# Attention scores from float32r products of split queries and keys, with the mask folded into the rotary product

## The chip, the cores and the metric

The kernel runs on one core of a Trainium2 chip. A core has a matrix engine (TensorE, PE in the profile, with weight loads as PEld), a vector engine (VectorE, DVE), a scalar engine (ScalarE, ACT), a general engine (GpSimd, POOL) and a queue for transfers (SyncE, SP). Each works through its own list of instructions in order and they meet at semaphores. Matrix products accumulate in PSUM, from where DVE or ACT move them to SBUF. The metric is the time of one launch on the device in microseconds.

## What is computed

Two layers of a transformer-like trunk on 256 tokens of 2048 features. Layer 0 is a convolution module and an MLP, layer 1 is latent attention and an MLP. Only the attention of layer 1 is touched. Its core, per block of 128 queries:

```python
s = (jnp.einsum('bqhd,bkhd->bhqk', qn, k_nope)
     + jnp.einsum('bqhr,bkr->bhqk', qp, k_pe)).astype(jnp.float32) * scale
q_chunk = (blk * Q_BLOCK + jnp.arange(Q_BLOCK)) // CHUNK
mask = k_chunk[None, :] <= q_chunk[:, None]
s = jnp.where(mask[None, None], s, -jnp.inf)
p = jax.nn.softmax(s, axis=-1).astype(v.dtype)
return jnp.einsum('bhqk,bkhd->bqhd', p, v)
```

There are 16 heads. A query has a part of 128 (qn) and a rotary part of 64 (qp); keys have a part of 128 per head (k_nope) and one rotary part of 64 that all heads share (k_pe). The mask lets a chunk of 64 queries see its own chunk of keys and the earlier ones, so query block 0 needs 128 keys and block 1 needs 256.

## The kernel before

Everything is float32. A long product is made of three float32r products (`mm3`): a float32r copy of each operand (its high part, written by ACT) and the difference to the original (its low part, by DVE) give high x high + low x high + high x low. Weights arrive by DMA as `raw`, are split by `split_half` in halves (L154 on ACT, L155 on DVE), and a list of units holds the order of all attention weights. `start_unit` notes that a unit has begun and `prefetch` then splits the unit two places ahead and loads one further on. Everything in the attention is issued in an order written out by hand.

The attention goes as follows. First the two down projections (`ckv` with the rotary key, then `cq`). During the second the rotary key is rotated by `rope` on DVE, copied twice side by side and transposed into `kpT` (L1141 to L1156). Then the heads, in four groups of four. The projections of a group are 14 pieces of about 1.4 us on PE each: four for queries (`qn_piece`), two for rotary queries (`qp_piece`, with `rope`), eight for keys and values (`kv_piece`); the pieces of group g+1 are spread over the four heads of group g, where they fill the time in which DVE and ACT do the softmax. `qp_turn` transposes the rotary queries of a group. In the last group, `o_piece` (parts of the output product) fills in instead.

One head in the loop at L1183: `scores` (L1037) makes the score products, the maxima on DVE (L1052, L1053) and the exponentials on ACT (L1055); one piece; `values` of the head before (L1075); `weights` (L1060: reciprocal and scaling on DVE); a prefetch; the other pieces, each with a prefetch; `weights_turn` (L1067), which transposes the probabilities on PE and copies them by ACT. In the scores the operands are plain float32:

```python
nc.tensor.matmul(o, qTs[g][:, i, ts], kTs[g][:, i, :n], start=True, stop=False)
nc.tensor.matmul(o, qpTs[g][half, i // 2, ts], kpT[half, :n], start=False, stop=False)
nc.tensor.matmul(o[:, n - CHUNK : n], mrow, mcol, start=False, stop=True)
```

The third adds -1e30 where the mask forbids, as a bfloat16 product over one partition. PSUM is cut into six accumulators (`acc`) and two tiles for transposes (`tr`), each handed out in turn.

Of the kernel before, what the change touches and what calls it, by code (L numbers as in the profile page):

```python
# [10 lines left out]
F32 = mybir.dt.float32  # L11
# [7 lines left out]
P = 128  # L19
D = 2048  # L20
KC = D // P
T = 2
S = T * P
# [13 lines left out]
PAD_CONST = 24  # L37
PAD_SMALL = 48
PAD_RIGHT = 48
PAD_KV = 40  # L40
PAD_O = 56
WB = 6
LOOK = WB // 2 - 1
# [29 lines left out]
def trunk_kernel(  # L73
# [54 lines left out]
    def nm(s):  # L128
        uid[0] += 1
        return f"{s}_{uid[0]}"  # L130
# [693 lines left out]
    with ExitStack() as cx:  # L824
# [3 lines left out]
        def rope(dst, src, t, nh):  # L828

            a, b = src[:, :, 0:HR], src[:, :, HR:DR]  # L830
            cb = cos[:, t : t + 1, :].broadcast_to([P, nh, HR])
            sb = sin[:, t : t + 1, :].broadcast_to([P, nh, HR])
            m = [at2.tile([P, 4, HR], F32, tag=f"m{i}", name=nm("m"))[:, :nh, :] for i in range(4)]
            nc.vector.tensor_tensor(m[0], a, cb, op=ALU.mult)
            nc.vector.tensor_tensor(m[1], b, sb, op=ALU.mult)
            nc.vector.tensor_tensor(m[2], b, cb, op=ALU.mult)
            nc.vector.tensor_tensor(m[3], a, sb, op=ALU.mult)
            nc.vector.tensor_tensor(dst[:, :, 0:HR], m[0], m[1], op=ALU.subtract)
            nc.vector.tensor_tensor(dst[:, :, HR:DR], m[2], m[3], op=ALU.add)


        mrow = at.tile([1, P], BF16, name="mrow")
        nc.vector.memset(mrow, 0.0)
        nc.vector.memset(mrow[:, 0:CHUNK], 1.0)
        mcol = at.tile([1, CHUNK], BF16, name="mcol")
        nc.vector.memset(mcol, NEG)

        HG = 4
        NG = H // HG
# [77 lines left out]
        kvl = at.tile([P, KR // P, S], F32R, name="kvl")  # L927
        qh = at.tile([P, QR // P, S], F32R, name="qh")
        ql = at.tile([P, QR // P, S], F32R, name="ql")
        kpT = at.tile([P, S], F32, name="kpT")  # L930
        pad_o = at.tile([P, PAD_O], F32, name="pad_o")
        nc.gpsimd.memset(pad_o, 0.0)
        oh = at.tile([P, H, S], F32R, name="oh")
# [18 lines left out]
        gp = []  # L952


        kTs, vvs, qTs, qps, qpTs = {}, {}, {}, {}, {}

        def kv_piece(g, i, c):

            key = ("kvu", g, i)
            if i == 0 and c == 0:  # L960
                kTs[g] = gp[0].tile([P, HG, S], F32, tag="kT", name=nm("kT"))
                vvs[g] = gp[0].tile([P, T, HG * DV], F32, tag="vv", name=nm("vv"))
            if c < 2:
                start_unit(key, c)
            po = acc_tile()
            if c < 2:
                o = po[:, :S]
                ns = slice(c * (DN + DV), c * (DN + DV) + DN)
                for j in range(NJ):
                    wh, wl = w_at(key, j)  # L970
                    nc.tensor.matmul(o, wh[:, ns], kvh[:, j, :], start=j == 0, stop=False)  # L971
                    nc.tensor.matmul(o, wh[:, ns], kvl[:, j, :], start=False, stop=False)  # L972
                    nc.tensor.matmul(o, wl[:, ns], kvh[:, j, :], start=False, stop=j == NJ - 1)  # L973
                nc.scalar.activation(kTs[g][:, 2 * i + c, :], o, AF.Copy)
            else:
                t = c - 2
                ts = slice(t * P, (t + 1) * P)
                o = po[:, : 2 * DV].rearrange("p (h n) -> p h n", h=2)
                for j in range(NJ):
                    wh, wl = (a.rearrange("p (h n) -> p h n", h=2)[:, :, DN:] for a in w_at(key, j))  # L980
                    mm3(o, kvh[:, j, ts], kvl[:, j, ts], wh, wl, j == 0, j == NJ - 1)
                nc.vector.tensor_copy(vvs[g][:, t, 2 * i * DV : 2 * (i + 1) * DV], po[:, : 2 * DV])

        def qn_piece(g, i):
            key = ("qn", g)
            if i == 0:
                qTs[g] = gp[0].tile([P, HG, S], F32, tag="qT", name=nm("qT"))
            if i < 2:
                start_unit(key, i)
            o = acc_tile()[:, :S]  # L990
            ns = slice(i * DN, (i + 1) * DN)
            for j in range(NJ):
                wh, wl = w_at(key, j)
                nc.tensor.matmul(o, wh[:, ns], qh[:, j, :], start=j == 0, stop=False)  # L994
                nc.tensor.matmul(o, wh[:, ns], ql[:, j, :], start=False, stop=False)
                nc.tensor.matmul(o, wl[:, ns], qh[:, j, :], start=False, stop=j == NJ - 1)
            nc.scalar.activation(qTs[g][:, i, :], o, AF.Copy)

        def qp_piece(g, t):
            key = ("qp", g)  # L1000
            start_unit(key, t)
            o = acc_tile()[:, : HG * DR]
            ts = slice(t * P, (t + 1) * P)
            for j in range(NJ):
                wh, wl = w_at(key, j)
                mm3(o, qh[:, j, ts], ql[:, j, ts], wh, wl, j == 0, j == NJ - 1)
            qps[g, t] = at2.tile([P, HG, DR], F32, tag="qp", name=nm("qp"))
            rope(qps[g, t], o.rearrange("p (h n) -> p h n", h=HG), t, HG)

        def qp_turn(g):  # L1010
            pt = tr_tile()
            for t in range(T):
                qp = qps.pop((g, t))
                for i in range(HG // 2):
                    nc.tensor.transpose(
                        pt[:, i * S + t * P : i * S + (t + 1) * P],
                        qp[:, 2 * i : 2 * i + 2, :].rearrange("p a b -> p (a b)"),
                        ident,
                    )
            qpTs[g] = gp[0].tile([P, HG // 2, S], F32, tag="qpT", name=nm("qpT"))  # L1020
            nc.vector.tensor_copy(qpTs[g].rearrange("p a b -> p (a b)"), pt)

        def kv_work(g):
            return [lambda i=i, c=c: kv_piece(g, i, c) for i in range(HG // 2) for c in range(4)]
# [3 lines left out]

        def group_work(g):
            kv = kv_work(g)  # L1030
            return q_work(g) + kv[:3] + [lambda: (qp_turn(g), kv[3]())] + kv[4:]


        sides = [(0, 0, P), (1, P, S)]
# [2 lines left out]
        def scores(h):  # L1037

            g, i = divmod(h, HG)
            half = slice((i % 2) * DR, (i % 2 + 1) * DR)  # L1040
            ss = scs[h] = acc_tile()
            mx = at2.tile([P, T], F32, tag="mx", name=nm("mx"))
            zs = zss[h] = at2.tile([P, T], F32, tag="zs", name=nm("zs"))
            pr = prs[h] = at2.tile([P, 3 * P], F32, tag="pr", name=nm("pr"))
            for t, at_, n in sides:
                o = ss[:, at_ : at_ + n]
                ts = slice(t * P, (t + 1) * P)
                nc.tensor.matmul(o, qTs[g][:, i, ts], kTs[g][:, i, :n], start=True, stop=False)  # L1048
                nc.tensor.matmul(o, qpTs[g][half, i // 2, ts], kpT[half, :n], start=False, stop=False)  # L1049
                nc.tensor.matmul(o[:, n - CHUNK : n], mrow, mcol, start=False, stop=True)  # L1050
            for t, at_, n in sides:
                nc.vector.tensor_reduce(mx[:, t : t + 1], ss[:, at_ : at_ + n], axis=AX.X, op=ALU.max)  # L1052
            nc.vector.tensor_scalar(mx, mx, scalar1=-SCALE, scalar2=None, op0=ALU.mult)  # L1053
            for t, at_, n in sides:
                nc.scalar.activation(  # L1055
                    pr[:, at_ : at_ + n], ss[:, at_ : at_ + n], AF.Exp, bias=mx[:, t : t + 1], scale=SCALE,
                    accum_out=zs[:, t : t + 1],
                )
# [42 lines left out]
        with tc.manual_schedule():  # L1101
# [26 lines left out]
            for k in range(KC):  # L1128
# [9 lines left out]
                if k == 3:  # L1138
                    normed(ckv, KR, sq)
                    kps = []  # L1140
                    for t in range(T):  # L1141
                        kp = at2.tile([P, 2, DR], F32, tag="kp", name=nm("kp"))
                        rope(kp[:, 0:1, :], ckv[:, t : t + 1, KR:], t, 1)
                        nc.vector.tensor_copy(kp[:, 1, :], kp[:, 0, :])
                        kps.append(kp)
                if k == 9:
                    to_T(ckv, 0, kvh_k, kvl_k, g_kv)
                if k == 11:
# [1 line left out]
                if k == 13:  # L1150
                    pt = tr_tile()
                    for t in range(T):
                        nc.tensor.transpose(
                            pt[:, t * P : (t + 1) * P], kps[t].rearrange("p a b -> p (a b)"), ident
                        )
                    nc.vector.tensor_copy(kpT, pt[:, :S])  # L1156
            cq = at.tile([P, T, QR], F32, tag="cx", name="cq")
            for t in range(T):
                nc.scalar.activation(cq[:, t, :], ps[t], AF.Copy, scale=r[:, t : t + 1])
# [15 lines left out]
            work = group_work(1)  # L1175
            warm(AF.Exp)
            work[0]()
            qp_turn(0)
            for w in work[1:3]:
                prefetch(1)  # L1180
                w()
# [1 line left out]
            for g in range(NG):  # L1183
                for i in range(HG):
# [3 lines left out]
                    todo, work = work[:n], work[n:]  # L1188
                    scores(h)
                    todo.pop(0)()  # L1190
                    if h > 0:
                        values(h - 1)
                    weights(h)
                    prefetch(1)
                    for w in todo:
                        w()
                        prefetch(1)
                    weights_turn(h)
                if g + 2 < NG:
                    work = group_work(g + 2)  # L1200
# [60 lines left out]
```

## Time and profile before

| | |
|---|---|
| time, median of 3 runs | 2034.71 us (2034.69 to 2035.07) |
| the profiled execution's own time | 2034.44 us |
| its span, first to last instruction | 2032.6 us |
| granted clock of PE | 0.999 |
| heads, from the first scores to the last | 1118.5 to 1251 us |
| PE records of the scores: L1048, L1049, L1050 | 64, 64 and 32 |
| transposes of the rotary queries, L1015 | 16 |

A line of the time view gives start in us, duration in us, engine, line, operation, output and inputs, shape and count; a bracket at its end is idle time before it and what ended it. Matmuls are pipelined, so their printed durations overlap and the distance of starts is the cost. A float32 product appears as two records and two weight loads, a float32r product as one. The page also names, per group of instructions, busy time, mean duration, and what ended the idle time before them.

### The profile page before, as it was taken

The numbers are of one execution on the slowest core, as the hardware profiler recorded it, in microseconds if no ns is written. First come the engines' busy times: TensorE is split into PE (matmuls) and PEld (weight loads), VectorE is DVE, ScalarE is ACT, GpSimd is POOL, SyncE is SP. The second block draws the span as 40 slices with busy tenths as digits, with TensorE's granted clock in tenths as the row PEclk, the third lists the DMA queues.
The fourth block names the chain that finished last, engine by engine and source line by source line (L and its number), as shares of the span: only waits on it lengthen the run. The fifth ranks groups of instructions, "written<-read, shape, count | busy, mean of one in ns | idle before, by whom it ended". The sixth has DMA issues, their size and how long they took to land.

```text
span 2032.6 us, 27882 instructions
## 1 busy us (share of the span) xinstructions
PE 2009.5 (99%) x11132; PEld 1747.1 (86%) x11132; DVE 1214.8 (60%) x1820; ACT 951.7 (47%) x1325; POOL 174.2 (9%) x101
## 2 busy tenths in 40 slices
PE   7999999999999999999999999999999999999998
PEld 7999888888888888888899887888888888888886
DVE  5999866665544465555446654665564455565454
ACT  5444655544433454444445444554443334454442
POOL 5887400000000000000000000000000000000000
PEclk9999999999999999999999999999999999999999
DMA  7555355665555665555555344566655566655552
GB/s 235 166 167 166 125 186 180 194 187 188 202 189 190 196 193 187 187 193 193 187 162 170 108 139 145 187 207 187 188 196 196 188 196 192 192 187 189 199 192 104
DMA packets 243268, 367.59 MB, mean 181 GB/s; under 512 B 15417, under 2 KB 89793, under 8 KB 242881
## 3 DMA queue, kind: packets, MB, share of 16 engines
q1 hardware_dynamic: 242400, 364.68, 56.0%
q8 instruction: 87, 1.43, 0.3%
q10 hardware_dynamic: 736, 1.12, 0.2%
q14 instruction: 45, 0.36, 0.0%
HBM read 363.68 MB, written 2.10 MB: 180 GB/s over the span
## 4 chain that ended last, share of the span: by engine, by line
PE 98%; DVE 1%; DMA 0%; ACT 0%; issue 0%; SPq 0%; DVEq 0%; ACTq 0%
PE acc L397 23%; PE acc L180 16%; PE acc L182 16%; PE acc L181 16%; PE acc L398 12%; PE acc L482 3%; PE acc L484 3%; PE acc L483 3%; PE sum L515 1%; PE acc L1049 1%; PE tr L237 1%; PE acc L1048 1%; PE acc L971 0%; PE acc L994 0%; PE acc L972 0%; PE acc L973 0%
## 5 line engine op out<-in xcount | busy, mean ns | idle before, releaser
L155 DVE TENSOR_TENSOR lo<-raw,hi 128x1024 fp32r<-128x1024 f32 (+1 forms) x628 | 755.2, 1206 | 685.1 <-ACT hi L154 673.3
L154 ACT ACTIVATE hi<-raw 128x1024 fp32r<-128x1024 f32 (+1 forms) x696 | 722.4, 1046 | 792.0 <-PE acc L181 458.3
L397 PE MATMUL acc<-xt,hi 128*128 128x512 f32 x2048 | 710.5, 390 | 0.0
L398 PE MATMUL acc<-xt,lo 128*128 128x256 f32 x2048 | 577.7, 282 | 0.0
L397 PEld LDWEIGHTS acc<-xt,hi 128*128 128x128 f32 x2048 | 384.4, 188 | 80.5
L180 PE MATMUL acc<-hi,gh 128*128 128x512 f32 x1024 | 398.6, 389 | 0.0
L182 PE MATMUL acc<-lo,gh 128*128 128x512 f32 x1024 | 398.4, 389 | 0.0
L181 PE MATMUL acc<-hi,gl 128*128 128x512 f32 x1024 | 398.4, 389 | 0.0
L398 PEld LDWEIGHTS acc<-xt,lo 128*128 128x128 f32 x2048 | 387.1, 189 | 0.1
L182 PEld LDWEIGHTS acc<-lo,gh 128*128 128x128 f32 x1024 | 192.2, 188 | 40.1
L180 PEld LDWEIGHTS acc<-hi,gh 128*128 128x128 f32 x1024 | 192.2, 188 | 39.7
L181 PEld LDWEIGHTS acc<-hi,gl 128*128 128x128 f32 x1024 | 192.2, 188 | 39.6
L549 DVE SCALAR_TENSOR_TENSOR sum<-ub,w_dw,sum 128x256 f32<-128x256 f32 x402 | 167.7, 485 | 4.9 <-ACT sum L518 2.9
L155 POOL TENSOR_TENSOR lo<-raw,hi 128x1024 fp32r<-128x1024 f32 x68 | 162.1, 2407 | 57.2 <-ACT hi L154 57.2
L482 PE MATMUL acc<-xt,hi 128*128 128x256 f32 x512 | 147.3, 288 | 0.0
L484 PE MATMUL acc<-xt,lo 128*128 128x256 f32 x512 | 143.2, 280 | 0.6 <-POOL lo L155 0.6
L483 PE MATMUL acc<-xt,hi 128*128 128x256 f32 x512 | 143.1, 279 | 0.0
L484 PEld LDWEIGHTS acc<-xt,lo 128*128 128x128 f32 x512 | 96.2, 188 | 0.8 <-POOL lo L155 0.8
L483 PEld LDWEIGHTS acc<-xt,hi 128*128 128x128 f32 x512 | 96.3, 188 | 0.6 <-DVE xt L193 0.2
L482 PEld LDWEIGHTS acc<-xt,hi 128*128 128x128 f32 x512 | 96.3, 188 | 0.4
L925 POOL MEMSET pad_kv<- 128x40 f32 x1 | 0.1, 132 | 772.6 <-PE acc L182 772.6
L405 ACT ACTIVATE v<-acc 128x256 f32<-128x256 f32 x128 | 46.4, 381 | 25.3 <-PE acc L398 25.3
(200 smaller groups left out, 1718.6 us busy)
## 6 DMA issues: line engine op xcount, KB each, us to landing
raw<-in_mlp_w SPq DMA_DIRECT2D x256, 1024.0 KB, 5.2
raw<-in_conv_w_pw SPq DMA_DIRECT2D x64, 512.0 KB, 4.9
raw<-in_conv_w_pw SPq DMA_DIRECT2D x16, 1024.0 KB, 5.1
raw<-in_mla_w_o SPq DMA_DIRECT2D x16, 1024.0 KB, 5.7
raw<-in_mla_w_kv_up SPq DMA_DIRECT2D x8, 1024.0 KB, 5.3
raw<-in_mla_w_in SPq DMA_DIRECT2D x8, 576.0 KB, 3.7
raw<-in_mla_w_in SPq DMA_DIRECT2D x4, 1024.0 KB, 5.0
raw<-in_mla_w_q_up SPq DMA_DIRECT2D x16, 256.0 KB, 3.2
```

Of the source, the lines that this page charges most:

```text
L154: nc.scalar.activation(hi, raw[:, js, :], AF.Copy)
L155: eng.tensor_tensor(lo, raw[:, js, :], hi.bitcast(F32), op=ALU.subtract)
L180: nc.tensor.matmul(ps, sh, mh, start=start, stop=False)
L181: nc.tensor.matmul(ps, sl, mh, start=False, stop=False)
L182: nc.tensor.matmul(ps, sh, ml, start=False, stop=stop)
L397: nc.tensor.matmul(ps[b], wh[:, bs], xhl(k), start=k == 0, stop=False)
L398: nc.tensor.matmul(ps[b][:, :S], wl[:, bs], xh(k), start=False, stop=k == KC - 1)
L405: nc.scalar.activation(v[:, b, :], o[:, S:], AF.Copy)
L482: nc.tensor.matmul(o, wh[:, bs], xh(k), start=k == 0, stop=False)
L483: nc.tensor.matmul(o, wh[:, bs], xl(k), start=False, stop=False)
L484: nc.tensor.matmul(o, wl[:, bs], xh(k), start=False, stop=k == KC - 1)
L549: nc.vector.scalar_tensor_tensor(out=out, in0=ubs[c][:, w : w + S], scalar=tap(c, w), in1=pcs[c], op0=ALU.mult, op1=ALU.add)
```

## The change

- Queries and keys are kept as a high and a low part (`parts_tile`, `in_parts`): the ACT copy out of PSUM now writes float32r, and a DVE subtraction writes the low part. The score product over 128 features becomes an `mm3`.
- The rotary part is stacked on partitions. `kpA` holds the high part of the rotary key twice, `qpA` the high part of the rotary query above its low part, so one product over 128 partitions gives two of the three terms. `kpB` holds the low part of the key in its upper 64 partitions and the mask values in the lower ones; `qpB` holds the high part of the query and the matching ones. Their product gives the third term and the mask. `mrow`, `mcol` and the bfloat16 product go away.
- `kpB` and the two `qpB` get their constant halves at the start of the attention: memsets into `scratch` and nine ACT copies.
- `qp_piece` also splits the rotated queries (`qhl`); `qp_turn` works in two visits of two heads each, with four transposes and two ACT copies per visit; the second visit goes with the next piece.
- In the loop over heads, `values` of the head before moves behind the pieces, to just ahead of `weights_turn`.
- Space: `rope`'s four temporaries have one buffer each, a pad is smaller, and the scratch space for dynamic DMA is cut to 1024 bytes, which shifts other tiles by 15,360 bytes.

```diff
-            m = [at2.tile([P, 4, HR], F32, tag=f"m{i}", name=nm("m"))[:, :nh, :] for i in range(4)]
+            m = [at2.tile([P, 4, HR], F32, tag=f"m{i}", name=nm("m"), bufs=1)[:, :nh, :] for i in range(4)]
...
-        kpT = at.tile([P, S], F32, name="kpT")
+        kpA = at.tile([P, S], F32R, name="kpA")
+        kpB = at.tile([P, S], F32R, name="kpB")
+        qpB = [at.tile([P, HG, S], F32R, name=f"qpB{i}") for i in range(2)]
+        mk, mq = scratch[:, :S], scratch[:, S:]
+        for m in (mk, mq):
+            nc.vector.memset(m[DR:, :], 0.0)
+        for t in range(T):
+            row = slice(DR + t * (P - DR) // 2, DR + t * (P - DR) // 2 + 1)
+            nc.vector.memset(mk[row, (t + 1) * P - CHUNK : (t + 1) * P], NEG)
+            nc.vector.memset(mq[row, t * P : t * P + CHUNK], 1.0)
+        nc.scalar.activation(kpB[DR:, :], mk[DR:, :], AF.Copy)
+        for i in range(2):
+            for j in range(HG):
+                nc.scalar.activation(qpB[i][DR:, j, :], mq[DR:, :], AF.Copy)
...
+        def in_parts(o, parts, i):
+            hi_part(o, parts[0][:, i, :])
+            lo_part(o, parts[0][:, i, :], parts[1][:, i, :])
...
-                nc.scalar.activation(kTs[g][:, 2 * i + c, :], o, AF.Copy)
+                in_parts(o, kTs[g], 2 * i + c)
...
-            nc.scalar.activation(qTs[g][:, i, :], o, AF.Copy)
+            in_parts(o, qTs[g], i)
...
-            qps[g, t] = at2.tile([P, HG, DR], F32, tag="qp", name=nm("qp"))
-            rope(qps[g, t], o.rearrange("p (h n) -> p h n", h=HG), t, HG)
-
-        def qp_turn(g):
+            qp = at2.tile([P, HG, DR], F32, tag="qp", name=nm("qp"))
+            rope(qp, o.rearrange("p (h n) -> p h n", h=HG), t, HG)
+            hl = qps[g, t] = at2.tile([P, HG, 2, DR], F32R, tag="qhl", name=nm("qhl"))
+            hi_part(qp, hl[:, :, 0, :])
+            lo_part(qp, hl[:, :, 0, :], hl[:, :, 1, :])
+
+        def qp_turn(g, m):
             pt = tr_tile()
-            for t in range(T):
-                qp = qps.pop((g, t))
-                for i in range(HG // 2):
+            for i in range(2):
+                for t in range(T):
                     nc.tensor.transpose(
                         pt[:, i * S + t * P : i * S + (t + 1) * P],
-                        qp[:, 2 * i : 2 * i + 2, :].rearrange("p a b -> p (a b)"),
+                        qps[g, t][:, 2 * m + i, :, :].rearrange("p a b -> p (a b)").bitcast(F32),
                         ident,
                     )
-            qpTs[g] = gp[0].tile([P, HG // 2, S], F32, tag="qpT", name=nm("qpT"))
-            nc.vector.tensor_copy(qpTs[g].rearrange("p a b -> p (a b)"), pt)
+            if m == 0:
+                qpAs[g] = gp[0].tile([P, HG, S], F32R, tag="qpA", name=nm("qpA"))
+            hs = slice(2 * m, 2 * m + 2)
+            o = pt.rearrange("p (i n) -> p i n", i=2)
+            nc.scalar.activation(qpAs[g][:, hs, :], o, AF.Copy)
+            nc.scalar.activation(qpB[g % 2][:DR, hs, :], o[:DR], AF.Copy)
...
-            return q_work(g) + kv[:3] + [lambda: (qp_turn(g), kv[3]())] + kv[4:]
+            turns = [lambda m=m: (qp_turn(g, m), kv[3 + m]()) for m in range(2)]
+            return q_work(g) + kv[:3] + turns + kv[5:]
...
-                nc.tensor.matmul(o, qTs[g][:, i, ts], kTs[g][:, i, :n], start=True, stop=False)
-                nc.tensor.matmul(o, qpTs[g][half, i // 2, ts], kpT[half, :n], start=False, stop=False)
-                nc.tensor.matmul(o[:, n - CHUNK : n], mrow, mcol, start=False, stop=True)
+                qT, kT = ([a[:, i, :] for a in x] for x in (qTs[g], kTs[g]))
+                mm3(o, qT[0][:, ts], qT[1][:, ts], kT[0][:, :n], kT[1][:, :n], True, False)
+                nc.tensor.matmul(o, qpAs[g][:, i, ts], kpA[:, :n], start=False, stop=False)
+                nc.tensor.matmul(o, qpB[g % 2][:, i, ts], kpB[:, :n], start=False, stop=True)
...
-                        kp = at2.tile([P, 2, DR], F32, tag="kp", name=nm("kp"))
-                        rope(kp[:, 0:1, :], ckv[:, t : t + 1, KR:], t, 1)
-                        nc.vector.tensor_copy(kp[:, 1, :], kp[:, 0, :])
+                        kp = at2.tile([P, 1, DR], F32, tag="kp", name=nm("kp"))
+                        rope(kp, ckv[:, t : t + 1, KR:], t, 1)
+                        hhl = at2.tile([P, 3, DR], F32R, tag="hhl", name=nm("hhl"))
+                        for i in range(2):
+                            hi_part(kp[:, 0, :], hhl[:, i, :])
+                        lo_part(kp[:, 0, :], hhl[:, 0, :], hhl[:, 2, :])
...
-            qp_turn(0)
+            for m in range(2):
+                qp_turn(0, m)
...
                     scores(h)
                     todo.pop(0)()
-                    if h > 0:
-                        values(h - 1)
                     weights(h)
                     prefetch(1)
                     for w in todo:
                         w()
                         prefetch(1)
+                    if h > 0:
+                        values(h - 1)
                     weights_turn(h)
```

## The prediction

> **What bounds the kernel now.** I read the page's busy shares and the chain of waits first.
>
> ```profile
> PE 2009.5 (99%) x11132; PEld 1747.1 (86%) x11132; DVE 1214.8 (60%) x1820; ACT 951.7 (47%) x1325; POOL 174.2 (9%) x101
> ...
> PE 98%; DVE 1%; DMA 0%; ACT 0%; issue 0%; SPq 0%; DVEq 0%; ACTq 0%
> ```
>
> TensorE (PE) sets the end: 98% of the chain is its own work, so a microsecond taken from PE is a microsecond of time, as long as nothing makes PE wait instead. The change acts in the attention heads; the stretch table there (busy us of PE, PEld, DVE, ACT, POOL; clock; DMA):
>
> ```profile
> 1118.00:1185.00 67.00, 67.00 (x470) 57.51 (x469) 39.48 (x107) 31.20 (x80) 0.00 (x0) 1.00 0.41 124
> 1185.00:1218.00 33.00, 33.00 (x233) 28.68 (x232) 20.85 (x53) 16.66 (x39) 0.00 (x0) 1.00 0.36 121
> 1218.00:1252.00 34.00, 34.00 (x157) 26.42 (x156) 15.31 (x29) 13.70 (x27) 0.00 (x0) 1.00 0.39 126
> ```
>
> PE never idles; DVE is busy some 60% until 1218 and 45% in the last group, whose filler work is long output products. Then the order in time on PE around one head's scores:
>
> ```profile
> 1140.61 0.49 PE L1071 MATMUL tr<-ident,pr 128*128 128x128 f32 x3
> 1140.94 0.39 PE L1048 MATMUL acc<-kT,qT 128*128 128x128 f32 x2
> 1141.26 0.48 PE L1049 MATMUL acc<-kpT,qpT 64*128 64x128 f32 x2
> 1141.67 0.20 PE L1050 MATMUL acc<-mcol,mrow 1*128 1x64 bf16 x1
> 1141.80 0.70 PE L1048 MATMUL acc<-kT,qT 128*128 128x256 f32 x2
> 1142.43 0.70 PE L1049 MATMUL acc<-kpT,qpT 64*128 64x256 f32 x2
> 1143.06 0.20 PE L1050 MATMUL acc<-mcol,mrow 1*128 1x64 bf16 x1
> 1143.19 0.39 PE L180 MATMUL acc<-hi,kvh 128*128 128x256 f32 x1
> 1143.41 0.28 PE L181 MATMUL acc<-hi,kvl 128*128 128x256 f32 x1
> 1143.53 0.28 PE L182 MATMUL acc<-lo,kvh 128*128 128x256 f32 x1
> ```
>
> Printed durations overlap; starts are what count. L181 to L182 is 0.117 us (1143.41 to 1143.53, rounded): the price of a split product of 256 columns. The scores run from 1140.94 to the L181 at 1143.41, less one ordinary product of 0.117: **2.35 us a head**. The transposes of a 128x128 tile:
>
> ```profile
> 1101.34 1.04 PE L237 MATMUL tr<-ident,cq 128*128 128x128 f32 x8
> 1102.13 0.36 PE L180 MATMUL acc<-hi,kvh 128*128 128x256 f32 x1
> 1102.33 0.28 PE L181 MATMUL acc<-hi,kvl 128*128 128x256 f32 x1
> ```
>
> Eight in about 0.87 us: 0.109 each, and 0.08 more when split products follow (0.20 to L181 where 0.117 is usual).
>
> **What the change takes from PE.** A head now has ten float32r products: five of 128 columns (query block 0) and five of 256. The 256 ones cost 0.117. No split product of 128 columns stands in this trace. Lower bound: the trend of 0.227 us at 512 columns and 0.117 at 256 gives 0.062 at 128. Upper bound: the float32 one, 0.32 (L1048 at 1140.94 to L1049 at 1141.26). I take 0.109, the transpose: same 4-byte weights of 128 columns to load, same 128 moving columns. So 5 x 0.117 + 5 x 0.109 = 1.13 a head. Entering them from transposes costs 0.08; the value products (L1080) now stand before the transposes instead of before split products and no longer pay theirs (0.20 where 0.117 is usual, 1129.75 to 1129.95). These cancel. Gain 16 x (2.35 - 1.13) = 19.5 us.
>
> The Trainium skill, page "TensorE: Matmul & The Clock Gate", section "Back-to-back issue gap", gives about 81 ns for a sustained load-and-multiply pair at N=128 and 131 ns at N=512. By its 81 ns the gain would be 16 x 5 x 0.028 = 2.2 us larger. At 512 columns this trace has 227 ns, not 131, so I stay with the row.
>
> **What it adds to PE.** The turn of the rotary queries makes 8 transposes a group instead of 4: 16 x 0.109 = 1.75. It is two visits instead of one: 4 x 0.08 = 0.3. Two more transposes for the keys: 0.2. Sum 2.3. PE work falls by **17.2 us**.
>
> **What it adds elsewhere.** Each of 32 query and key tiles gets a subtraction on DVE of the kind of L191 (0.42 busy, 0.35 from start to start). Each of 8 rotary pieces gets an ACT copy and a DVE subtraction (some 0.4 each with the hand-over). Each group gets four ACT copies of 512 columns (0.52 apart) in place of one DVE copy (0.69). Half the turn's pieces and most subtractions are in the first three groups. Ahead of the heads there are nine ACT copies of 256 columns for mask and padding (0.27 apart, 2.4 us), six memsets (0.11 each), and some small copies for the rotary key. They delay weight splits that are prepared two units, four halves of 2.72 us, before use; ACT idles 2.0 us in each 2.72. Cost nothing, at most 2.4 if that lead were gone. The eight subtractions in the projections of group 0 (DVE 22.3 busy of 33 us) I also cost at nothing, at most 0.65, since the query's second part ends 0.65 later than before and each product waits for its own slice.
>
> The heads are another matter. DVE and ACT work in the written order, and a split of weights waits on ACT, then on DVE. Before, head 1 was already late:
>
> ```profile
> 1127.39 1.22 DVE L155 TENSOR_TENSOR lo<-raw,hi 128x1024 fp32r<-128x1024 f32 x1
> 1128.53 0.62 DVE L1052 TENSOR_REDUCE mx<-acc 128x1 f32<-128x128 f32 x2
> ...
> 1131.47 0.55 DVE L1065 TENSOR_SCALAR pr<-pr,zs 128x128 f32<-128x128 f32 x2
> ```
>
> ```profile
> 1129.45 0.37 ACT L1055 ACTIVATE pr<-acc,mx 128x128 f32<-128x128 f32 x1 [3.34 <-DVE mx L1053]
> ```
>
> Its maxima waited behind a split, and its weights were ready at 1132.0, 0.8 us before PE turned them (1132.82). I followed both queues with these start-to-start times: rope 1.2 (six of 0.20), maxima to exponentials 0.9, exponentials 0.95, reciprocal and scaling 0.75, split 0.97 on ACT and 1.15 on DVE (half that for 512 columns).
> - First turn: rope of t=0 ends at 1113.55. Then ACT copy (0.4); the split behind it on ACT (0.5) and on DVE (0.6); rope of t=1 (1.3); ACT copy and DVE subtraction (0.8): ready at 1117.2. The second transpose ran at 1115.4. Wait 1.8.
> - Head 0: ACT then has a half split, the table load (1.28), one query copy, four turn copies (2.1), a split, a copy, a split, a copy: to 1123.6. DVE's maxima stand behind the last subtractions, at 1124.75; exponentials 1125.65; another copy and subtraction; scaling ends 1128.0. PE, with scores of 1.13 and three pieces of 1.4, is there at 1126.3. Wait 1.7.
> - Head 1: from 1128.0 DVE has two ropes, each followed by copy, subtraction and split: 2 x 3.7. Maxima at 1135.45, exponentials done 1137.3, key copy and subtraction 0.6, scaling 0.75: 1138.65. PE reaches the value products at 1133.7, waits 1.1 for the weights' copy behind a split on ACT, does them (0.65), and waits 3.2 more. Wait 4.3.
> - Groups 1 and 2: their second head carries two ropes, four splits and two key subtractions, 12.5 us for DVE with its waits, against 7.75 on PE (1.13 + 4 x 1.4 + 0.65 + 0.33). The next head's maxima start 4.8 late; exponentials (1.7) and two turn copies (1.0) follow, and a turn's PSUM tile comes free 1.6 after PE wants it. Wait 1.6, twice.
> - The other heads have slack; in group 3 three output products of 2.7 us cover each softmax.
>
> New waits: 1.8 + 1.7 + 4.3 + 3.2 = **11.0 us**. What is queued behind DVE in them is the next head's maxima, and PE waits for those. Net -17.2 + 11.0 = -6.2. Span 2032.6 becomes 2026.4; with 1.8 around it (profiled time 2034.44) 2028.2; the median of the runs stands 0.27 above the profiled time: **2028.5 us**. Own range 2024 to 2034 (waits 6.5 to 16.5).
>
> **Rivals.**
> - *The waits don't come.* DVE and ACT catch up, the moved value products help: 2034.7 - 17.2 = 2017.5. For it: before, no wait of PE on DVE in the heads, and busy sums below 85% of the shorter span. Against: the late maxima above, with 0.8 left. Chance 0.12.
> - *The narrow product stays as dear as float32.* If 128 columns in float32r cost 0.32, a head costs 2.19, the gain is 2.6, transposes take 2.3, and the waits, one microsecond of PE longer per head, still some 8: +7.7, 2042.4, slower. It decides from x with 16 x 5 x (x - 0.109) = 6.2, x = 0.187. For it: nothing here shows the narrow product, and every split product of this kernel is 256 columns or wider. Against: float32 shows two weight loads per product (x64 for 32 products) where the split one has one. Chance 0.18.
> - *DVE and ACT become the bound in groups 0 to 2.* DVE needs some 25 us a group of 29 on PE. If hand-overs cost each of the 11 other heads a further microsecond: 2028.5 + 11 = 2039.5. For it: two engines in lockstep. Against: half the heads carry under 7 us of DVE work. Chance 0.10.
>
> **How the numbers follow.** Forecast 0.60. About 0.2%, 4 us, is what a measurement of this kernel can tell from no change: the bounds are 2030.6 and 2038.8. Faster: 0.65 of the forecast, all of the first rival: 0.51. Slower: three quarters of the second, 0.6 of the third: 0.20. The rest, 0.29, within. Range 2019 to 2041: it takes in the waits from 1.5 us on, the two costs taken at nothing, and narrow products up to about 0.27.
>
> **What would show it.** Narrow products 0.11 us apart and 1.13 us a head; PE waits on DVE at the first turn, at heads 0 and 1, and at heads 6 and 10, none in group 3. Wrong if the narrow products stand 0.2 or more apart, or if PE in 1113 to 1210 waits under 5 us or over 17.

## The result and the profile after

| | before | after |
|---|---|---|
| median | 2034.72 us (2034.37 to 2035.19, 20 runs) | 2031.57 us (2031.05 to 2033.79, 20 runs) |
| profiled execution's own time | 2034.44 us | 2031.51 us |
| its span | 2032.6 us | 2029.7 us |
| granted clock of PE | 0.999 | 0.997 |

The ratio is 0.9985 (95% interval 0.9979 to 0.9992): faster by some 3 us, half of what was forecast. By the prediction's own bounds, which take 2030.6 to 2038.8 us for no difference, 2031.57 lies in the middle, to which it gave 0.29, and not in "faster", to which it gave 0.51; the 20 runs of each kernel do tell the difference from zero. The busy shares and the chain of waits of the kernel after:

```profile
PE 1997.2 (98%) x11150; PEld 1749.3 (86%) x11150; DVE 1227.8 (60%) x1858; ACT 964.5 (48%) x1364; POOL 174.0 (9%) x101
...
PE 95%; DVE 3%; ACT 1%; issue 0%; DMA 0%; SPq 0%; DVEq 0%; ACTq 0%
```

PE lost 12.3 us of busy time, and DVE and ACT, which held 1% of the chain, now hold 4%. The order in time on PE around the scores of head 0 (start and duration in us; starts are what count):

```profile
1121.80 0.22 PE L180 MATMUL acc<-kTh,qTh 128*128 128x128 f32 x1
1121.86 0.28 PE L181 MATMUL acc<-kTh,qTl 128*128 128x128 f32 x1
1121.97 0.27 PE L182 MATMUL acc<-kTl,qTh 128*128 128x128 f32 x1
1122.08 0.27 PE L1073 MATMUL acc<-kpA,qpA 128*128 128x128 f32 x1
1122.19 0.27 PE L1074 MATMUL acc<-kpB,qpB 128*128 128x128 f32 x1
1122.30 0.33 PE L180 MATMUL acc<-kTh,qTh 128*128 128x256 f32 x1
...
1122.95 0.28 PE L1010 MATMUL acc<-qh,hi 128*128 128x256 f32 x1
```

The narrow products stand 0.11 us apart, and ten products take 1.15 us (1121.80 to 1122.95), where the old scores took 2.35. So PE's work fell as computed. What was given back is in the table of PE's waits (us in total, times, longest):

```profile
PE tr L1095 <- DVE pr L1089: 4.1, 2, 2.6
PE tr L1095 <- ACT qpB L1044: 2.8, 2, 1.4
PE tr L1034 <- DVE qhl L191: 2.3, 1, 2.3
```

The turn of the weights (L1095) waits for DVE's scaling in heads 0 and 1 (1.5 and 2.6 us) and for a PSUM tile that ACT's copies of the rotary queries empty late in heads 6 and 10 (1.4 each); the first turn of rotary queries (L1034) waits 2.3 for their low part. Before, PE had none of these waits. The stretch table (busy us of PE, PEld, DVE, ACT, POOL; clock; DMA):

```profile
1118.00:1185.00 67.00, 61.14 (x478) 59.82 (x479) 45.72 (x123) 39.34 (x97) 0.00 (x0) 0.95 0.38 111
1185.00:1218.00 33.00, 31.30 (x258) 30.47 (x257) 24.21 (x64) 20.19 (x48) 0.00 (x0) 1.00 0.39 128
1218.00:1252.00 34.00, 34.00 (x174) 28.98 (x173) 18.36 (x39) 15.97 (x33) 0.00 (x0) 1.00 0.48 155
```

The first row holds a surprise beside the idle time: the clock is 0.95 there, and was 1.00. Finer stretches of the same view find it:

```profile
1126.58:1129.99 3.41, 1.91 (x17) 1.68 (x16) 2.12 (x11) 1.19 (x5) 0.00 (x0) 1.00 0.68 154
1129.99:1133.40 3.41, 3.41 (x18) 3.41 (x18) 2.35 (x7) 1.36 (x2) 0.00 (x0) 0.50 0.02 5
1136.82:1140.23 3.41, 0.79 (x6) 0.47 (x6) 2.08 (x8) 2.67 (x8) 0.00 (x0) 1.00 0.62 177
1140.23:1143.64 3.41, 3.41 (x19) 3.41 (x18) 3.41 (x7) 1.34 (x3) 0.00 (x0) 0.50 0.38 139
```

PE is granted half its clock twice, for 3.41 us each, after stretches in which it idled 1.5 and 2.6 us. The first time DVE is behind anyway (the turn of head 1 comes 10.45 us after its first score product, and 10.44 in e2_warm below, where the clock holds); the second time PE's own work is on the path (scores of head 2: 2.18 us instead of 1.24). The chain of waits in between, in order of time (head 1), shows who was late:

```profile
1130.26 0.42 ACT qhl L186
1130.67 0.95 ACT hi L154
1131.65 1.23 DVE lo L155
...
1134.17 0.42 ACT qhl L186
1134.59 0.96 ACT hi L154
1135.57 1.23 DVE lo L155
1136.79 0.54 DVE mx L1076 x2
1137.36 0.18 DVE mx L1077
1137.83 0.65 ACT pr L1079 x3
1138.48 0.28 ACT kTh L186
1138.79 0.42 DVE kTl L191
1139.32 0.30 DVE pr L1089
1139.66 0.70 PE tr L1095 x3
```

Work passes from ACT to DVE and back, and both weight splits (L154, L155) stand in the queues ahead of the maxima (L1076), though nothing needs them yet.

### The profile page after: what moved, and what is told of

Read it like the earlier page. It is cut to its first block, busy times and chain, and to the rows that moved or that the text cites. A ratio compares the mean times of both kernels' runs of the same rounds, so it can differ in the third digit from the quotient of the medians.

```text
span 2029.7 us, 28001 instructions
## 1 busy us (share of the span) xinstructions
PE 1997.2 (98%) x11150; PEld 1749.3 (86%) x11150; DVE 1227.8 (60%) x1858; ACT 964.5 (48%) x1364; POOL 174.0 (9%) x101
## 4 chain that ended last, share of the span: by engine, by line
PE 95%; DVE 3%; ACT 1%; issue 0%; DMA 0%; SPq 0%; DVEq 0%; ACTq 0%
PE acc L397 23%; PE acc L180 16%; PE acc L181 16%; PE acc L182 16%; PE acc L398 12%; PE acc L482 3%; PE acc L484 3%; PE acc L483 3%; PE sum L515 1%; PE tr L237 1%; DVE lo L155 1%; DMA xs<-in_x 0%; ACT hi L154 0%; PE acc L1011 0%; PE acc L1012 0%
## 5 line engine op out<-in xcount | busy, mean ns | idle before, releaser
L155 DVE TENSOR_TENSOR lo<-raw,hi 128x1024 fp32r<-128x1024 f32 (+1 forms) x628 | 755.6, 1206 | 682.7 <-ACT hi L154 669.8
L154 ACT ACTIVATE hi<-raw 128x1024 fp32r<-128x1024 f32 (+1 forms) x696 | 722.8, 1046 | 790.2 <-PE acc L181 453.8
L155 POOL TENSOR_TENSOR lo<-raw,hi 128x1024 fp32r<-128x1024 f32 x68 | 161.9, 2404 | 57.7 <-ACT hi L154 57.7
```

Source lines behind the costliest of these rows:

```text
L154: nc.scalar.activation(hi, raw[:, js, :], AF.Copy)
L155: eng.tensor_tensor(lo, raw[:, js, :], hi.bitcast(F32), op=ALU.subtract)
```

## The experiments

Each was timed beside the kernel before. All but e8_before_values are edits of the kernel after (2031.57 us).

**Is it the amount of DVE work?** The splits' subtractions in the heads go to GpSimd.

```diff
-                parts[n, h] = split_half(raws[n], h, nc.vector)
+                on_pool = pieces["qp", 1] <= n < pieces["o", 0]
+                parts[n, h] = split_half(raws[n], h, nc.gpsimd if on_pool else nc.vector)
```

> The changed kernel, but the subtraction of every weight split issued from the last rotary piece of group 0 to the end of group 2 goes to GpSimd (2.4 us each there, against 1.2 on DVE; GpSimd idles in the attention). My theory: PE waits because DVE's queue is late, and a late split that stands ahead of the next maxima is what makes it so. Then the waits at head 1 and at heads 6 and 10 all but vanish (3.9 and 1.8 and 1.8 us now), the first turn waits 1.0 instead of 2.1, head 0 about 0.9, and without long gaps the granted clock stays at 1.00: 2031.6 - 8 - 1.6 = about 2022. Rival, ACT is the late one: it keeps all its copies and splits, the waits stay within 1 us of now, and the time is about 2030. Second rival: GpSimd and DVE get in each other's way and splits come late: 2033 or more.

Measured: 2036.36 us (2036.1 to 2038.78), ratio 1.0009 (1.0 to 1.0018). A miss by 14 us, and what the second rival said (2033 or more). The order in time on DVE and POOL in this kernel:

```profile
1132.73 0.28 DVE L837 TENSOR_TENSOR m<-acc,sin 128x128 f32<-128x128 f32 x1
...
1132.83 2.38 POOL L155 TENSOR_TENSOR lo<-raw,hi 128x1024 fp32r<-128x1024 f32 x1 [5.14 <-PE acc L1075]
...
1132.92 2.43 DVE L838 TENSOR_TENSOR qp<-m,m 128x128 f32<-128x128 f32 x1
...
1135.28 0.28 DVE L839 TENSOR_TENSOR qp<-m,m 128x128 f32<-128x128 f32 x1
```

L838 reads two SBUF tiles and takes 0.28 us elsewhere; here it lasts 2.43 and ends when the GpSimd subtraction does. DVE was hardly relieved: from 1118 us to the first head of group 3 (1221 us, here 1226) 21.9 us of subtractions left it, and its busy time fell by only 6.8 us (71.8 to 65.0). So this run does not tell whether the amount of work matters. The next kernel leaves out the low parts of queries and keys.

```diff
-            return [gp[0].tile([P, HG, S], F32R, tag=tag + c, name=nm(tag + c)) for c in "hl"]
+            return [gp[0].tile([P, HG, S], F32R, tag=tag + "h", name=nm(tag + "h"))] * 2
...
-            lo_part(o, parts[0][:, i, :], parts[1][:, i, :])
```

> The changed kernel without the 32 subtractions that make the low parts of queries and keys: the score products read the high parts in their place, so two of the three terms are not the right ones; PE does the same number of products of the same shapes. Theory: few of these subtractions stand in the late chains (two in head 0, one in head 1, two each before heads 6 and 10), so PE's waits shrink by some 2.6 us, and 1.6 more if the clock then holds: 2027.5 to 2029. Rival, this added DVE work is what makes all the waits: 2021.

Measured: 2029.15 us (2027.79 to 2030.75), ratio 0.9972 (0.9961 to 0.9982). With 32 subtractions of 0.42 us gone (13 us of DVE), 2.4 us are won; 7.6 us of waits are left in the heads and the first turn, where there were 9.2. That is just outside the expected 2027.5 to 2029 (half clock came here too, for 6.8 us in the heads), and far from the rival's 2021. So the amount of work in these subtractions is the smaller part. The next two runs ask for the hand-overs and the order.

**Is it the hand-over?** The high part of the rotary query is written by DVE, so that DVE does not wait for ACT between rotation and subtraction.

```diff
-            hi_part(qp, hl[:, :, 0, :])
+            nc.vector.tensor_copy(hl[:, :, 0, :], qp)
```

> The changed kernel, but the high part of the rotary queries is written by DVE instead of ACT, so the rotary pieces lose one trip from DVE to ACT and back, and ACT's next split no longer stands behind that trip. DVE gets 0.3 us more per piece. Theory, the trip is dear because queues stand behind it: the first turn waits 1.2 less, head 1 about 2.5 less, heads 6 and 10 about 0.5 less each; 2031.6 - 4.5 = 2027, and up to 1.6 less if the clock holds. Rival, DVE is simply full: its 2.4 us more of work makes the waits longer, 2032 to 2034.

Measured: 2026.38 us (2024.74 to 2026.87), ratio 0.9956 (0.9944 to 0.9969), 5.2 us less than the kernel after for one line, and the rival falls. "Scores to turn" is from the end of the scores (as in the prediction: the second product behind them less 0.117 us) to the first transpose of the weights. It falls from 5.90 to 4.79 us in head 0, from 8.75 to 7.62 in head 1, from 7.71 to 6.85 in heads 6 and 10, and the first turn waits 1.8 instead of 2.3: 4.4 us in all. No half clock appears in the heads, though PE still idles 2.6 us in head 1. The trace is of the quickest of five executions, 2024.74 us; the others took 2025.08 to 2026.87, so it is not shown how much of the 5.2 us is shorter waits and how much the clock.

**Is it the order?** In groups 0 to 2 the weight splits go behind the scaling (`weights`) instead of behind the pieces.

```diff
-                    prefetch(1)
+                    prefetch(9 if g < NG - 1 else 1)
                     for w in todo:
                         w()
-                        prefetch(1)
+                        if g == NG - 1:
+                            prefetch(1)
```

> The changed kernel with one thing reordered: in groups 0 to 2 the weight splits that a head's pieces call for are issued together right behind the next head's scaling, instead of one behind each piece, so none stands ahead of the next maxima. Same work on every engine. Theory: what PE waits for is the order, not the amount: the maxima of head 1 start 4 us earlier, those of heads 6 and 10 too, these waits vanish (3.9, 1.8 and 1.8 us), and with them the half clock in head 2 (1.6): 2031.6 - 8.5 = about 2023. The waits at the first turn (2.1) and head 0 (1.7) stay. Rival, DVE is simply short of time: the waits only move to heads 2, 7 and 11, 2029 or more.

Measured: 2026.96 us (2026.67 to 2028.84), ratio 0.9963 (0.9951 to 0.9976). Between theory and rival. Head 1 needs 5.73 us from scores to turn, heads 6 and 10 need 5.89: their waits are gone or down to 0.7. But the table of PE's waits has new ones:

```profile
PE tr L1034 <- DVE qhl L191: 2.3, 1, 2.3
PE acc L989 <- DVE lo L155: 1.6, 2, 0.8
PE acc L987 <- ACT hi L154: 1.3, 2, 0.7
```

In heads 5 and 9 the first key piece now finds its weights unsplit (scores to turn 8.29 and 8.28 us instead of 6.29). Here the first turn's gap was followed by half clock too, at 1118.81.

**What is the half clock worth?** Dummy transposes of the identity fill PE's gaps in heads 0 and 1 (`keep_warm`, 40 in all).

```diff
+                    if h == 1:
+                        keep_warm(ident, 8)
                     if h > 0:
                         values(h - 1)
+                    if h < 2:
+                        keep_warm(ident, (12, 20)[h])
```

> The changed kernel with idle PE time filled: 12 transposes of a constant tile ahead of the probabilities' turn in head 0, 8 ahead of the value products and 20 ahead of the turn in head 1. They use nothing and nobody reads them; they end before the data that PE waits for. Theory: the granted clock fell to half from 1130.0 to 1133.4 and from 1140.2 to 1143.6 because PE had stood still 1.5 and 2.6 us just before; with the gaps filled it stays at 1.00, head 2 costs 1.24 for its scores instead of 2.18, and the time falls by some 1.6 us to about 2030.0. Rival, the clock falls for another reason, or transposes don't count as work for it: no difference, 2031.6, or up to 1 us more if the fill is too long.

Measured: 2029.72 us (2029.57 to 2030.19), ratio 0.9975 (0.9965 to 0.9984): 1.85 us less. The clock stays at 1.00 in the heads, the scores of head 2 take 1.24 us, and the waits at the first turn and in heads 6 and 10 are as before (2.2 and 2.8 us). Work that computes nothing makes the kernel faster.

**What is the move of the value products worth?** First put back behind the first piece in the kernel after:

```diff
                     todo.pop(0)()
+                    if h > 0:
+                        values(h - 1)
                     weights(h)
...
-                    if h > 0:
-                        values(h - 1)
                     weights_turn(h)
```

> The changed kernel with the value products put back right after the first piece, as before. Theory: in the heads that wait, PE waits for the same DVE work either way, the value products only wait earlier (in head 1 for the weights' copy, about 3 us, and then two pieces of cover are left), and in the other heads nothing changes: 2031.6 within 1 us. Rival, the move is what gives the softmax its cover: 3 us or more slower, 2034.6 or above.

Measured: 2034.02 us (2031.75 to 2036.91), ratio 0.9994 (0.9985 to 1.0003), about 2.4 more in the median. But the eleven executions fall into two bunches: five took 2031.75 to 2031.94 us at a granted clock of 0.997, which is what the kernel after takes, and six took 2034.02 to 2036.91 at 0.994 to 0.996. The first bunch is where the theory had it, the second close to the rival. The trace is of one of the six (2034.86 us). Its table of PE's waits:

```profile
PE acc L1104 <- ACT pT L1097: 8.0, 3, 3.9
```

The copies of the turned weights (`pT`) stand behind splits on ACT, and value products issued early wait for them with the pieces behind them in PE's queue. PE is granted half its clock for 10.2 us in the heads of this trace, against 6.8 in the kernel after. So the early value products do wait in a new place, but 2.4 us is not shown to be the price of it: five executions of eleven lost nothing, and the trace is of none of these. The move alone, in the kernel before:

```diff
-                    if h > 0:
-                        values(h - 1)
                     weights(h)
...
+                    if h > 0:
+                        values(h - 1)
                     weights_turn(h)
```

> The kernel before with only the value products moved to just ahead of the probabilities' turn. Theory: nothing waits there, but the step from float32 value products to split products, 0.08 us, falls away in 15 heads: 2034.7 - 1.2 = 2033.5. Rival: that step isn't saved, or the softmax had used that place: 2034.7 or slower.

Measured: 2034.26 us (2033.78 to 2035.79), ratio 0.9998 (0.9989 to 1.0007): nothing that can be told from zero. In its trace the heads, from the first scores to the last turn, take 0.7 us less (141.3 against 142.1), of the 1.2 expected, but they begin 0.78 us later. What the move is worth in the kernel after stays open.

**Everything that helped, together.** e4's line and e5's order, both rotary pieces of group 0 ahead of their splits, and the table load earlier.

```diff
-            for w in work[6:] + q_work(0):
+            warm(AF.Exp)
+            for w in work[6:] + q_work(0)[:-2]:
                 w()
                 prefetch()
+            for w in q_work(0)[-2:]:
+                w()
+            prefetch()
...
-            warm(AF.Exp)
```

> That reordering, the rotary high part on DVE, both rotary pieces of group 0 ahead of their splits, and the table for the exponentials loaded before the query pieces of group 0 instead of after. Theory: the first turn waits 0.7 instead of 2.1, head 0 nothing, no other head waits, and nearly all of the 17.2 us taken from PE shows: 2034.7 - 17.2 + 1.5 = about 2019. Rival, another wait stands right behind those removed (ACT's copies of the turned queries, PSUM tiles): 2021 to 2024.

Measured: 2024.26 us (2024.12 to 2024.61), ratio 0.9948 (0.9936 to 0.9961), a miss by 5, and just above the rival's 2021 to 2024, though not by the waits that the rival named: the waits in heads 5 and 9 grew to 1.6 us each and the first turn kept 1.2. The next two take these one at a time. Splits are held back only where a head would be late:

```diff
+            late = lambda g, i: g == NG - 1 or (g > 0 and i == 0)
...
-                    prefetch(9 if g < NG - 1 else 1)
+                    prefetch(1 if late(g, i) else 9)
                     for w in todo:
                         w()
-                        if g == NG - 1:
+                        if late(g, i):
                             prefetch(1)
```

> Against the kernel after this has everything of e6_best, but the weight splits are held back to behind the scaling only where the head carries rotary pieces or the mask of group 0 has them near (all heads of group 0, the second to fourth of groups 1 and 2); in the first heads of groups 1 and 2 (heads 4 and 8) each piece is followed by one half split, as in the kernel after. Theory: the two waits of 1.6 us in e6_best on the low part of a weight split (heads 5 and 9) come from the splits held back in heads 4 and 8, so both go and heads 5 and 9 need 6.3 us from scores to turn instead of 8.2: 2024.3 - 3.2, less up to 0.5 for the time that the later head had used, 2021.0 (2020.5 to 2021.8). Rival: the splits in heads 4 and 8 are then in front of the maxima of heads 5 and 9, and the waits only change their kind: 2023.5 or more, with a wait of PE on DVE pr in heads 5, 6, 9 or 10.

Measured: 2021.24 us (2020.93 to 2023.1), ratio 0.9935 (0.9921 to 0.9949); heads 5 and 9 need 6.30 and 6.29 us again. And one more piece ahead of the first turn:

```diff
             work[0]()
+            prefetch(1)
+            work[1]()
             for m in range(2):
                 qp_turn(0, m)
-            for w in work[1:3]:
-                prefetch(1)
-                w()
+            prefetch(1)
+            work[2]()
```

> Like e9_selective, and two pieces of group 1 instead of one stand before the first turn of the rotary queries, one behind it. Theory: the wait of 1.2 us that PE has there on the low part of the rotary query (qhl) is covered by the piece of 1.4 us, and the turn's copies by ACT still come in time for the rotary products of head 0, since the split products of 128 features stand ahead of them: 1.2 less than e9_selective, 2019.8 (2019.0 to 2020.6). Rival: the wait moves to the rotary products of head 0 (PE L1073 on ACT qpA or qpB): same as e9_selective within 0.5.

Measured: 2019.95 us (2019.64 to 2021.55), ratio 0.9928 (0.9915 to 0.994). Both theories hold within 0.25 us. In this best version all of PE's waits in the heads come to 1.4 us:

```profile
PE tr L1095 <- DVE pr L1089: 1.0, 3, 0.4
PE tr L1095 <- ACT qpB L1044: 0.4, 2, 0.2
```

It does the same products as the kernel after; only the order, and the engine of one copy, differ. It takes 14.8 us less than the kernel before, where the change as it was made brought 3.15. The same order was not tried on the kernel before, but that one has no waits of PE in the heads that an order could remove.

## Why the prediction was right, and where it was not

The forecast was 2028.5 us and a change of -6.2; measured were 2031.57 and, between the two profiled executions, -2.9. By its steps:

| step | predicted, us | measured, us |
|---|---|---|
| gain of the scores | 19.5 | 18.7 |
| added transposes | 2.3 | 2.1 |
| wait at the first turn | 1.8 | 2.3 |
| head 0 | 1.7 | 1.5 |
| head 1 | 4.3 | 4.3 |
| heads 6 and 10 | 3.2 | 2.8 |
| head 11 | 0 | 0.3 |
| half clock in head 2 | 0 | 1.6 |
| start of the attention | 0 | 0.8 |

The measured terms sum to -18.7 + 2.1 + 10.9 + 0.3 + 1.6 + 0.8 = -3.0.

- *The gain.* Right in mechanism; the taken 0.109 for the narrow product is 0.11 in the trace. The rival that it stays at 0.32 fell with the first view. By the 81 ns that the Trainium skill, page "TensorE: Matmul & The Clock Gate", section "Back-to-back issue gap", gives for N=128 the step would have been further off; the row decides. The sum over 16 heads is some 17.8 for the scores (without the two half-clock stretches) and 0.06 a head in the step into them: 0.8 less than taken. The new scores are 1.15 to 1.35 us a head and the old ones 2.30 to 2.47, where one head had stood for all.
- *The transposes.* The prediction counts 0.109 for each and 0.08 more for the step behind them. Its lines give 0.87 us for eight with that step in it (1101.34 to 1102.33 less 0.117), so 0.3 of its 2.3 was counted twice.
- *The new waits.* All came where they were placed, and 11.0 predicted stands against 10.9; that the sums agree so well is in part luck, as the first turn cost 0.5 more and heads 6 and 10 together 0.4 less. In head 1 the 4.3 is made of 2.6 us idle and 1.7 in which PE worked at half clock: its pieces took that much longer, and DVE would have been late anyway (e2_warm). The wait of 1.1 us for the weights' copy, the first of the two that the prediction has there, did not come (0.3 in e2_warm). That DVE's queue is what is late there is shown by e4_dvehi and e5_order, which shorten it by 1.1 and 3.0 us. "The other heads have slack" and "none in group 3" held, but for 0.3 us in head 11. So did the point named for failure: PE idles 9.2 us in these waits, between 5 and 17.
- *What failed.* The sum assumed that a wait costs its length. The step "Net -17.2 + 11.0" lacks a term: after a gap PE may be granted half its clock, and in head 2 that is 1.6 us on the path. e2_warm took it away and won 1.85. That is half of what the forecast was off; the rest is the gain and the start.
- *Costs taken at nothing.* The heads' first new piece starts 0.77 us later than before. Of this 0.34 is there from 300 us on, ahead of all that changed, and is variation between executions: e2_warm, e4_dvehi and e5_order, which so far have the instructions of the kernel after, lie within 0.1 us of the kernel before at 1026 us, and e8_before_values, whose instructions up to the heads are those of the kernel before, starts its heads 0.78 late. The two added transposes of the keys are 0.22, which the table has twice, so its terms agree with -2.9 within some 0.3. The last 0.18 arise at the transposes of `cq`, which wait for DVE's scaling of `cq`; it starts 0.8 later, and two of the eight new subtractions now stand ahead of it. The prediction had named that cost and put it at nothing, at most 0.65. The memsets and the nine copies (1045 to 1051 us) delay PE by nothing that shows: it is 0.34 late at 1040 us and 0.36 at 1085.
- *The moved value products* were counted only for their 0.08 us steps. Whether they are worth more in the kernel after is open (e3_values).
- *The other rivals.* DVE and ACT did not become the bound. The prediction's sum for that has 11 other heads; groups 0 to 2 have eight beside the four late ones, and all groups twelve. Of these twelve ten are within 0.1 us of their old time from scores to turn; head 2 (+1.0) holds added transposes and half clock, head 11 has +0.3. The waits did come, so 2017.5 did not; but e10_first_turn, with the waits planned away, ends 2.5 us from it, of which 1.4 are the waits that are left.

## What to carry to other kernels

When a change moves work from the bounding engine to engines with 40% idle time, sum their instructions head by head, in queue order: the share of idle time says nothing about one late instruction behind a split that nobody needs yet. Then hold back what is not urgent, but only where something urgent follows; held back everywhere, it is late itself. A copy that lets one engine do two steps in a row can be worth more than the balance between two engines.

## What the hardware showed that was not expected

*Half clock after short gaps.* In five traces (the kernel after, e1_pool, e3_values, e5_order, e7_nolow) PE falls to 0.50 in the heads, eight times in all. In traces with several such drops they start 10.24 us (the kernel after, e1_pool) or 40.96 us (e3_values) apart, which is 3 and 12 times 3.41. Each trace also has a drop at the end of its span, 2 to 5 us after PE has finished, and it too lies on this grid (2024.28 in the kernel after, 262 such stretches behind the first). Cut into stretches of 3.41 us on that grid, the seven stretches at full clock with 2.0 us or more of idle PE were each followed by half clock; of those with 1.5 to 1.93 us, one was (1126.58, above) and six were not. Two rows of e3_values show both sides:

```profile
1172.22:1175.63 3.41, 1.39 (x11) 1.16 (x10) 3.24 (x5) 2.95 (x6) 0.00 (x0) 1.00 0.26 39
1175.63:1179.04 3.41, 3.41 (x17) 3.33 (x16) 2.39 (x7) 1.66 (x7) 0.00 (x0) 0.50 0.98 350
1206.35:1209.76 3.41, 1.48 (x11) 1.43 (x12) 3.41 (x7) 1.88 (x4) 0.00 (x0) 1.00 0.56 160
```

PE idles 2.02 us in the first and drops; it idles 1.93 in the third, and the clock stays. So what a gap costs depends on where it falls: the same 2.3 us at the first turn cost a drop in e5_order and none in the kernel after, where the grid cuts it in two (0.41 and 1.85). In e4_dvehi the 2.58 us of idle PE in head 1 cost none either: on the grid of the drop at its end (2016.12 us) they fall into two stretches, 1.90 and 0.68. That the bunches of times in e3_values and in e4_dvehi come from where the grid lay would fit, but is not shown. The Trainium skill, page "TensorE: Matmul & The Clock Gate", section "What's actually happening", speaks of a free-running window of 3413 ns and of half clock after a window that is idle. The length and the free running agree with these starts; that the whole window must be idle does not, as 2.0 us of it were enough.

*A DVE that stands still beside GpSimd.* In e1_pool the means of DVE's work from SBUF to SBUF in the heads rose from 282 to 1122 ns (L838) and from 317 to over 480 (the scaling), while rotations that read PSUM (L834 to L837) stayed at 0.28 us. The Trainium skill, page "SBUF — State Buffer", section "SBUF: two separate sides", calls it an exclusive lock on a pair of ports that DVE and GpSimd share, which agrees with 2.43 us beside 2.38. The second rival of e1_pool had said that the two would get in each other's way; had the rule been weighed, that would have been the forecast.
